# Ten of 22 up-projection pairs as seven half-size products, weight sums on GpSimd, and a first unit fed input by input

## The chip, the cores and the metric

One core of one Trainium2 chip runs the whole program. The metric is the device time of one execution, in microseconds (us). An engine is named as in the profile: PE is TensorE, ACT ScalarE, DVE VectorE, POOL GpSimd, SP the engine that issues the DMAs.

## What is computed

One inference step of a two-layer decoder trunk over 520 token columns: 512 of a prompt and 8 of a sample group. Everything is float32.

```python
def layer(x, ...):
    proj = rmsnorm(x, g_mix) @ w_in            # 1024 -> 5376: u_a v_a q k v gate_a gate_b
    a_out = chunk_spatial_gate(gelu(u_a), rmsnorm(gelu(v_a), g_v), w_s, b_s)
    b_out = merged dilated window attention of q, k, v (three pairs of window and dilation)
    merged = sigmoid(gate_a) * (a_out @ w_a_proj) + sigmoid(gate_b) * (b_out @ w_b_proj)
    x = x + merged @ w_o
    up = rmsnorm(x, g_ffn) @ w_up              # 1024 -> 2 * 2816
    c = conv_b + causal depthwise conv of 3 taps over up
    c_gate, c_val = split(c)
    return x + (silu(c_gate) * c_val) @ w_down # 2816 -> 1024
```

## The kernel before

**Layout and precision.** Activations lie transposed: 128 features on the partitions, 520 tokens along a row, as `x[:, k]` for the eight blocks k of the 1024 features. Each float32 operand of a dense product is split into a high part in the reduced format that PE takes (`act.copy` on ACT) and the rest as a low part (a subtraction on DVE). `triple` (L333) issues three products for one pair of operands, high by high, high by low and low by high, and each for the two halves of the tokens, 260 columns at a time. One output block of 128 features over 1024 inputs takes 8 x 3 x 2 = 48 matmuls; an up pair (one block of values, one of gates) takes 96.

**Order of the work.** `groups` lists the dense products in program order: for each layer the projection of w_in, the gate pairs ("ga", "gb") with w_a_proj and w_b_proj as the loop over j and the tuple `mix` have it, w_o, and then `ffn`: 22 up pairs, with the blocks of w_down for the first three pieces of the hidden features put between them, and the last piece at the end. `loads` and `blocks` follow from it. Weight blocks of 128 x 512 come by DMA into nine `raw` buffers; `split` (L260) makes their high and low parts, in a ring of six (`RING`), as soon as the block six before has been used. Everything else (norm statistics, attention, the gating branch, state columns) is written as generators in lanes; `pump` takes the next step of a lane between matmuls when its due time has come in a running count of PE time. The tile scheduler then fixes each engine's queue; within a queue instructions run in order.

**Norms.** `Norm.feature` splits gain times x into high and low before the norm's factor is known; `Norm.rms` gets that factor from the sums of squares by matmuls with ones (L472), a power on POOL (L137), transposes (L483) and a copy to `rbc`. The factor is multiplied in when a product's accumulators are taken out of PSUM by DVE (`normed` L1142, `copied` L1079). In the first unit, three blocks of layer 0 (`lows_last`), the high weights go first and the low ones last.

**Seven products.** `dense2` (L393) holds a second form for a pair of blocks: two halves of the inputs by two blocks of outputs against two halves of the inputs by two halves of the tokens, as seven products of half size in place of eight, with sums of weight blocks (`summed`, L264, on POOL), sums of normalised inputs (`Norm.operands`), and sums of accumulators when they are taken out. `SEVEN`, the tuple of pairs that take it, is empty, so neither `summed` nor `operands` runs.

**The conv.** `up_conv` (L1378) takes an up block through ACT (L1384) and DVE (L1386, twice, and L1389); `conved` multiplies value and gate and splits the result (L1402, L1403, L568, L569). `a_branch` (L1166) loads the spatial weights w_s and multiplies them by the causal mask (L1172) in its first step.

Of the kernel before, what the change touches and what calls it, by code (L numbers as in the profile page):

```python
# [18 lines left out]
D = 1024  # L19
T = 520  # L20
# [59 lines left out]
NSTD = 3  # L80

SEVEN = ()
# [6 lines left out]
def step_kernel(ctx: ExitStack, tc: tile.TileContext, a, o):  # L89
# [58 lines left out]

    groups = []
# [7 lines left out]
    mix = ("g0", "g1", "b0", "g2", "b1", "b2", "g3", "b3", "b4", "b5", "b6", "b7")  # L157
    for l in range(DEPTH):
# [12 lines left out]
        for p in (2, 1, 0):  # L171
            c = [off + p * 256 + h * 128 for off in (O_Q, O_K, O_VV) for h in range(2)]
            if p == 2:
                n = 3
                one(w_in, 0, 8, *c[:n])
# [9 lines left out]
        for j in range(5):  # L185
            if j < 4:
                two(("ga", j), w_in, O_GA + j * 256, O_GA + j * 256 + 128)
            for i in (2 * j - 2, 2 * j - 1) if j else ():
                one(a["w_a_proj"][l], 0, 4, i * 128)
        for g, j in mix:  # L190
            j = int(j)
            if g == "g":
                two(("gb", j), w_in, O_GB + j * 256, O_GB + j * 256 + 128)
            else:
                one(a["w_b_proj"][l], 0, 2, j * 128)
# [27 lines left out]
    for g, grp in enumerate(groups):  # L223
        if grp[0] == "s":
# [3 lines left out]
            continue  # L228
        _, w, k0, nk, cs = grp
        for k, k1 in steps(nk):  # L230
# [5 lines left out]
          "pin": False}  # L236
    at = {b: i for i, b in enumerate(blocks)}

# [3 lines left out]
    def load_raw():  # L242
# [3 lines left out]
        dma(r[:, :nk], w[k0 * 128 : (k0 + nk) * 128, c0 : c0 + 128].rearrange("(k p) m -> p k m", p=128))  # L246
# [8 lines left out]
    def split(eng=dve):  # L255
# [9 lines left out]
        if groups[g][0] == "u":  # L265
# [12 lines left out]
        with urgent():  # L278
            act.copy(hi[:, :nk], r)  # L279
            eng.tensor_tensor(lo[:, :nk], r, hi[:, :nk].bitcast(F32), op=ALU.subtract)  # L280
# [3 lines left out]
    def feed():  # L284
        while st["split"] < len(blocks) and (st["split"] < RING or st["split"] - RING in st["used"]):
# [21 lines left out]
    def pump(force=False):  # L307

        while True:
            e = [q + [n] for n, k in LANES.items() for q in tasks[n][:k]]  # L310
# [20 lines left out]
    def finish(*lanes):  # L331
        while any(tasks[n] for n in lanes):
            pump(True)  # L333

    def triple(w, x, bank, start, stop, which=(0, 1, 2)):

        pump()
# [15 lines left out]
    def dense(xs, unit, lows_last=False):  # L353
# [7 lines left out]

        def taken(j):
            finish("n")
            with urgent():
                unit(j, *banks[j])

        held = {}
        ks = steps(nk)
        for k0, k1 in ks:
            for j, c in enumerate(cs):  # L370
                held[j, k0] = block(g, (k0, c))
            last = k1 == nk and not lows_last
            for js in [[j] for j in range(len(cs))] if last else [range(len(cs))]:
                for k in range(k0, k1):
                    for j in js:
                        hi, lo = held[j, k0]
                        triple((hi[:, k - k0], lo[:, k - k0]), xs[k], banks[j], k == 0, k == nk - 1,
                               (0, 1) if lows_last else (0, 1, 2))
                if last:
                    used(g, (k0, cs[js[0]]))  # L380
                    taken(js[0])
            if not last and not lows_last:
                for c in cs:
                    used(g, (k0, c))
        for j, c in enumerate(cs) if lows_last else ():
            for k0, k1 in ks:
                feed()
                hi, lo = held[j, k0]
                for k in range(k0, k1):
                    triple((hi[:, k - k0], lo[:, k - k0]), xs[k], banks[j], False, k == nk - 1, (2,))  # L390
                used(g, (k0, c))
            taken(j)

    def dense2(norm, unit, done):
# [5 lines left out]
        while norm.seven and (not norm.xn or (groups[st["g"]][0] == "s" and tasks["x"])):  # L400
            pump(True)
# [38 lines left out]
    class Norm:  # L440


        def __init__(self, gofs, ksum=8):
            self.gofs = gofs
            self.xs = []
            self.ssum = [tmp() for _ in range(2 if ksum < 8 else 1)]
            self.ksum = ksum

        def feature(self, k):
            hi = tmp(T, F32R)  # L450
            lo = tmp(T, F32R)
# [1053 lines left out]
```

## Time and profile before

| | |
|---|---|
| Runs | 1583.2, 1587.14 (median), 1588.96 us |
| Profiled execution | 1582.85 us, of which the span of the trace is 1581.0 us |
| PE matmuls busy | 1558.7 us, 99% of the span, 12985 matmuls |
| DVE busy | 1065.0 us, 67% |
| ACT busy | 713.4 us, 45% |
| POOL busy | 70.9 us, 4% |
| DMA | 164.37 MB, 104 GB/s over the span |

PE is busy throughout, but a matmul's end is modelled and matmuls overlap, so its rate is read from how many of them fit in a stretch rather than from the busy share. The other engines' shares are means over stages that differ much, and a stage is read on its own.

### The profile page before, as it was taken

To read this page: it belongs to the slowest core of one execution; us is meant where nothing else is said; L and a number is where in the kernel's file an instruction comes from. 1 tells how busy PE (TensorE), PEld (TensorE's weight loads), DVE (VectorE), ACT (ScalarE), POOL (GpSimd) and SP (SyncE) were. 2 spreads that over 40 slices of the span, in tenths; PEclk is the share of its full clock that TensorE was granted. 3 is DMA by queue.
4 is the path that set the end of the run, shared out by engine and by line. 5 is a ranking of instruction groups with operands and counts; after the bars stand their busy time and mean duration, and the time that the engine had idled before them with its cause. 6 is when DMAs were issued, how large, how long until landed. Compare 5 with 4: busy or idle time off the path is not lost.

```text
span 1581.0 us, 33056 instructions
## 1 busy us (share of the span) xinstructions
PE 1558.7 (99%) x12985; PEld 1532.2 (97%) x12985; DVE 1065.0 (67%) x2353; ACT 713.4 (45%) x1513; POOL 70.9 (4%) x58
## 2 busy tenths in 40 slices
PE   7999999999999999999999999999999999999999
PEld 6999899999999999999999998999999999999998
DVE  5677868966576665665648686788666766667563
ACT  4564535434454343433545645453444444334342
POOL 0102010000000000000001030100000000000000
PEclk9999999999999999999999999999999999999999
DMA  8343333533323323323344343334333233242321
GB/s 220 110 121 112 108 108 96 162 95 108 87 83 87 101 76 105 96 85 92 102 121 133 94 131 89 112 111 144 94 107 88 78 88 96 83 117 78 101 75 66
DMA packets 299163, 164.37 MB, mean 104 GB/s; under 512 B 18439, under 2 KB 292631, under 8 KB 298991
## 3 DMA queue, kind: packets, MB, share of 16 engines
q1 hardware_dynamic: 299007, 162.26, 35.2%
q8 instruction: 102, 1.67, 0.4%
q14 instruction: 54, 0.44, 0.1%
HBM read 154.66 MB, written 10.36 MB: 104 GB/s over the span
## 4 chain that ended last, share of the span: by engine, by line
PE 95%; DVE 2%; DMA 1%; ACT 1%; SPq 1%; issue 0%; DVEq 0%
PE acc L342 87%; PE tp L843 2%; PE tp L891 1%; PE tp L881 1%; PE tp L800 1%; PE tp L342 1%; PE tp L1239 0%; DVE t L1047 0%; DMA t<-in_x_prompt_dram 0%; PE tp L793 0%; PE tp L826 0%; PE tp L950 0%; PE tp L1214 0%; PE tp L825 0%; DVE t L454 0%
## 5 line engine op out<-in xcount | busy, mean ns | idle before, releaser
L342 PE MATMUL acc<-t,whi 128*128 128x260 f32 x7744 | 1295.5, 285 | 1.4 <-DVE t L1079 1.4
L342 PEld LDWEIGHTS acc<-t,whi 128*128 128x128 f32 x7744 | 1087.6, 189 | 6.9 <-DVE t L1079 2.5
L342 PE MATMUL acc<-t,wlo 128*128 128x260 f32 x3872 | 837.9, 284 | 0.0
L342 PEld LDWEIGHTS acc<-t,wlo 128*128 128x128 f32 x3872 | 619.9, 189 | 2.4 <-issue 0.7
L279 ACT CAST whi<-raw 128x512 fp32r<-128x512 f32 (+2 forms) x536 | 312.0, 583 | 660.4 <-PE acc L342 527.3
L280 DVE TENSOR_TENSOR wlo<-raw,whi 128x512 fp32r<-128x512 f32 (+2 forms) x536 | 341.5, 638 | 170.4 <-ACT whi L279 158.9
L1079 DVE TENSOR_TENSOR t<-acc,t 128x260 f32<-128x260 f32 x296 | 112.5, 421 | 121.9 <-PE acc L342 121.9
L1386 DVE SCALAR_TENSOR_TENSOR t<-t,cwc,t 128x511 f32<-128x511 f32 (+1 forms) x176 | 131.6, 749 | 44.6 <-ACT t L1384 44.4
L1361 DVE TENSOR_TENSOR x<-acc,x 128x260 f32<-128x260 f32 x128 | 48.8, 421 | 37.8 <-PE acc L342 37.7
L1384 ACT ACTIVATE t<-t,vcol,cwc 128x520 f32<-128x520 f32 x88 | 72.1, 819 | 0.0
L137 POOL TENSOR_TENSOR rr<-ss,mhalf 128x8 f32<-128x8 f32 (+1 forms) x30 | 56.2, 1873 | 286.0 <-DVE ss L756 211.8
L569 DVE TENSOR_TENSOR t<-t,t 128x520 fp32r<-128x520 f32 (+1 forms) x84 | 51.8, 617 | 21.7 <-ACT t L568 21.4
L568 ACT CAST t<-t 128x520 fp32r<-128x520 f32 (+1 forms) x84 | 47.3, 563 | 40.5 <-DVE t L1403 18.2
L866 ACT ACTIVATE t<-t,stat 128x128 f32<-128x128 f32 (+1 forms) x96 | 40.0, 419 | 9.1 <-DVE stat L863 8.7
L137 POOL TENSOR_TENSOR rc<-ms,mhalf 128x5 f32<-128x5 f32 x4 | 4.7, 1173 | 748.4 <-DVE ms L477 748.4
L1382 ACT COPY ut<-t 128x10 f32<-128x10 f32 x88 | 18.4, 209 | 34.9 <-DVE t L1079 34.4
L1403 DVE TENSOR_TENSOR t<-t,t 128x520 f32<-128x520 f32 x44 | 30.6, 696 | 1.6 <-ACT t L1402 1.3
L843 PE MATMUL tp<-t 64*128 64x128 f32 x192 | 30.5, 293 | 0.0
L857 DVE TENSOR_TENSOR t<-tp,cst 128x256 f32<-128x256 f32 (+1 forms) x48 | 22.4, 484 | 11.9 <-PE tp L843 11.7
L1402 ACT ACTIVATE t<-t 128x520 f32<-128x520 f32 x44 | 28.1, 639 | 2.2 <-DVE t L1389 0.6
L1363 DVE SCALAR_TENSOR_TENSOR x<-acc,x 128x260 f32<-128x260 f32 x32 | 12.3, 422 | 23.9 <-PE acc L342 23.9
L843 PEld LDWEIGHTS tp<-t 64*128 64x128 f32 x192 | 22.5, 187 | 4.7 <-issue 1.7
(185 smaller groups left out, 996.2 us busy)
## 6 DMA issues: line engine op xcount, KB each, us to landing
raw<-in_w_up_dram SPq DMA_DIRECT2D x176, 256.0 KB
raw<-in_w_in_dram SPq DMA_DIRECT2D x168, 256.0 KB
raw<-in_w_down_dram SPq DMA_DIRECT2D x96, 192.0 KB
t<-in_cache_kv_w_dram SPq DMA_DIRECT2D x48, 256.0 KB
raw<-in_w_o_dram SPq DMA_DIRECT2D x32, 256.0 KB
raw<-in_w_a_proj_dram SPq DMA_DIRECT2D x16, 256.0 KB
raw<-in_w_down_dram SPq DMA_DIRECT2D x32, 128.0 KB
out_dram<-t SPq DMA_DIRECT2D x15, 256.0 KB
```

The lines of the kernel that those rows point to most:

```text
L137: pool.tensor_tensor(out, in_, mhalf[: in_.shape[0], :n], op=ALU.pow)
L279: act.copy(hi[:, :nk], r)
L280: eng.tensor_tensor(lo[:, :nk], r, hi[:, :nk].bitcast(F32), op=ALU.subtract)
L342: mm = pe.matmul(b, wi, xi[:, h * H2 : h * H2 + H2], start=start and i == 0, stop=stop and i == 2,)
L568: act.copy(hi, src)
L569: dve.tensor_tensor(lo, src, hi.bitcast(F32), op=ALU.subtract)
L843: pe.matmul(sc[h2][:, hp * K + s * 128 : hp * K + s * 128 + 128], qkT[rows, hp], kt[rows, 2 + hp], start=True, stop=True,)
L866: act.activation(S[:, hp], S[:, hp], AF.Exp, bias=nmx[:, i : i + 1], accum_out=stat[:, 4 + i : 5 + i])
L1079: dve.tensor_tensor(v2(g)[:, h], acc, n.rb[:, h], op=ALU.mult)
L1361: dve.tensor_tensor(xm, acc, xm, op=ALU.add)
L1384: act.activation(cv, up, AF.Identity, scale=cwc[:, 2, i : i + 1], bias=vcol[:, 32 + i : 33 + i])
L1386: dve.scalar_tensor_tensor(cv[:, s:TP], up[:, : TP - s], cwc[:, j, i : i + 1], cv[:, s:TP], op0=ALU.mult, op1=ALU.add)
```

## The change

`SEVEN` gets the ten up pairs 9, 10, 12, 13, 15, 16, 18, 19, 20 and 21 of each layer, and `NSTD` goes from 3 to 7. In each of these pairs the seven products run, POOL makes four sums of weight blocks, and the splits go from four blocks to seven. `Norm.operands`, which makes the normalised inputs and their sums, runs in steps between the matmuls of the first up pairs; the pairs 7, 8, 11, 14 and 17 use the normalised inputs too, and ACT copies their results out instead of DVE multiplying them.

The first unit of layer 0 (`dense_first`) takes inputs one at a time: the transposes and splits of block k + 1 run while the products of block k - 1 do, and three weight blocks come in one buffer per input. The mask of w_s (L1221, two instructions a layer) comes a step later than its loads, the two lanes of layer 0 start later, and `mix` now orders gate pairs, w_a_proj and w_b_proj in one list.

```diff
-NSTD = 3
-SEVEN = ()
+NSTD = 7
+SEVEN = tuple(("up", i) for i in (9,10,12,13,15,16,18,19,20,21))
+DELAY0 = 1.0
...
-    mix = ("g0", "g1", "b0", "g2", "b1", "b2", "g3", "b3", "b4", "b5", "b6", "b7")
+    mix = "g0 g1 g2 a0 a1 g3 a2 a3 h0 a4 a5 h1 h2 b0 a6 b1 b2 a7 b3 h3 b4 b5 b6 b7".split()
...
+        if grp[0] == "k":
+            loads.extend((grp[1], k, 3, grp[2:]) for k in range(8))
+            blocks.extend((g, k) for k in range(8))
+            continue
...
-    def dense(xs, unit, lows_last=False):
+    def dense(xs, unit):
...
+    def dense_first(feature, norm, unit):
+        st["g"] += 1
+        banks = [[acc_tile(), acc_tile() if j < 2 else tps()[:, :H2]] for j in range(3)]
+        w = []
+        xsq = [tmp(), tmp()]
+        for k in range(8):
+            if 0 < k < 7:
+                for j in range(3):
+                    hi, lo = w[k - 1]
+                    triple((hi[:, j], lo[:, j]), norm.xs[k - 1], banks[j], k == 1, False)
+                used(0, k - 1)
+            st["limit"] = k + 1
+            with tc.high_priority(3 * URGENT):
+                feature(k)
+                w.append(block(0, k))
+                norm.square(k, xsq[k % 2])
+        norm.finish(DELAY0)
+        st["limit"] = 0
+        for j in range(3):
+            for k in (6, 7):
+                hi, lo = w[k]
+                triple((hi[:, j], lo[:, j]), norm.xs[k], banks[j], False, k == 7)
...
+            finish("n")
+            with urgent():
+                unit(j, *banks[j])
...
             if self.seven:
-                add("x", self.operands(), delay + 0.1)
+                add("x", self.operands(), delay + 16.0)
...
-                yield -0.7
+                yield -4.0
...
+    def first_feature(k):
...
+        def columns(k):
+            t = tps()
+            for b in range(4):
+                pe.transpose(t[:, b * 128 : b * 128 + 128], xin[k][:, b], ident)
+            kept(act.copy(x[:, k, :TP], t))
+        if k == 0:
+            columns(0)
+        if k < 7:
+            columns(k + 1)
+        norm.split(k)
...
             for i in range(2):
                 dma(ws[i], a["w_s"][l, 4 * i : 4 * i + 4].rearrange("g t s -> t g s"))
+            yield -4.0
+            for i in range(2):
                 dve.tensor_tensor(
...
-        add("v", a_branch(), 12.0)
-        add("s", attn_samples(), 12.0)
+        add("v", a_branch(), 12.0 if l else 20.0)
+        add("s", attn_samples(), 12.0 if l else 24.0)
```

**PE at the start of the program, before** (L603 transposes inputs, L608 and L613 the sample rows and gains, L342 is the dense product):

```order
L603 MATMUL tp_120<-cst,t_83 128x128 x4
L608 MATMUL tp_126<-cst,t_86 128x8 x4
L608 MATMUL tp_126<-cst,t_87 128x8 x4
L613 MATMUL tp_126<-cst,t_78 128x16
L603 MATMUL tp_151<-cst,t_95 128x128 x4
L603 MATMUL tp_164<-cst,t_97 128x128 x4
L603 MATMUL tp_185<-cst,t_103 128x128 x4
L603 MATMUL tp_198<-cst,t_105 128x128 x4
L342 MATMUL acc_288<-t_138,whi_143 128x260
L342 MATMUL acc_289<-t_138,whi_143 128x260
L342 MATMUL acc_290<-t_138,whi_147 128x260
```

**and with the change** (L658 transposes inputs, L644 and L650 the gains and sample rows, L362 is the dense product):

```order
L644 MATMUL tp_170<-cst,t_78 128x16
L650 MATMUL tp_173<-cst,t_85 128x8 x4
L658 MATMUL tp_179<-cst,t_87 128x128 x4
L658 MATMUL tp_185<-cst,t_95 128x128 x4
L362 MATMUL acc_162<-t_191,whi_195 128x260
L362 MATMUL acc_163<-t_191,whi_195 128x260
L362 MATMUL acc_164<-t_191,whi_195 128x260
L362 MATMUL acc_165<-t_191,whi_195 128x260
L362 MATMUL acc_166<-t_191,whi_195 128x260
L362 MATMUL tp_167<-t_191,whi_195 128x260
L658 MATMUL tp_218<-cst,t_100 128x128 x4
L658 MATMUL tp_252<-cst,t_105 128x128 x4
```

Before, five groups of transposes stand ahead of the first dense matmul; now two do, and the transposes of later inputs follow between the matmuls.

**DVE at the end of the first norm, before** (L462 adds squares, L1172 masks w_s, L280 makes low weights, L476 and L477 begin the norm's factor):

```order
L462 TENSOR_TENSOR t_82<-t_82,t_229 128x520
L462 TENSOR_TENSOR t_82<-t_82,t_242 128x520
L1172 TENSOR_TENSOR t_414<-t_414,cst 128x512
L462 TENSOR_TENSOR t_82<-t_82,t_255 128x520
L1172 TENSOR_TENSOR t_415<-t_415,cst 128x512
L280 TENSOR_TENSOR wlo_436<-raw_294,whi_435 128x512
L280 TENSOR_TENSOR wlo_473<-raw_296,whi_472 128x512
L476 TENSOR_SCALAR ms_394<-tp_388 128x4
L477 TENSOR_SCALAR ms_394<-tp_388 8x1
```

**and with the change** (the same steps are L502, L299, L514 and L515; L493 makes the low part of an input; L1189 takes the first results out):

```order
L493 SCALAR_TENSOR_TENSOR t_419<-x,vcol,t_418 128x520
L299 TENSOR_TENSOR wlo_423<-raw_127,whi_422 128x384
L502 TENSOR_TENSOR t_82<-t_82,t_169 128x520
L299 TENSOR_TENSOR wlo_498<-raw_300,whi_497 128x512
L299 TENSOR_TENSOR wlo_502<-raw_342,whi_501 128x512
L299 TENSOR_TENSOR wlo_506<-raw_378,whi_505 128x512
L299 TENSOR_TENSOR wlo_510<-raw_414,whi_509 128x512
L514 TENSOR_SCALAR ms_448<-tp_442 128x4
L515 TENSOR_SCALAR ms_448<-tp_442 8x1
L512 MEMSET ms_10963 128x1
L1189 TENSOR_TENSOR t_463<-acc_162,t_83 128x260
```

The mask of w_s stood between the last two adds of squares; now it comes after the first results have been taken out.

**DVE where the splits of up pair 10 begin, before** (L280 low weights, L1079 takes a result out, L1386 and L1389 the conv):

```order
L280 TENSOR_TENSOR wlo_7409<-raw_7277,whi_7408 128x512
L280 TENSOR_TENSOR wlo_7443<-raw_7307,whi_7442 128x512
L1079 TENSOR_TENSOR t_7478<-acc_7416,t_5693 128x260
L1079 TENSOR_TENSOR t_7478<-acc_7417,t_5693 128x260
L280 TENSOR_TENSOR wlo_7473<-raw_7348,whi_7472 128x512
L1386 SCALAR_TENSOR_TENSOR t_7481<-t_7478,cwc,t_7481 128x511
L1389 TENSOR_TENSOR t_7481<-t_7481,hc_280 128x8
L1386 SCALAR_TENSOR_TENSOR t_7481<-t_7478,cwc,t_7481 128x510
L280 TENSOR_TENSOR wlo_7514<-raw_7366,whi_7513 128x512
L1079 TENSOR_TENSOR t_7549<-acc_7487,t_5693 128x260
L1079 TENSOR_TENSOR t_7549<-acc_7488,t_5693 128x260
L280 TENSOR_TENSOR wlo_7544<-raw_7394,whi_7543 128x512
```

**and with the change** (`sum` tiles come from POOL; L457 and L462 take a half-size product out with a sum):

```order
L299 TENSOR_TENSOR wlo_7554<-sum_7397,whi_7553 128x512
L457 TENSOR_TENSOR t_7538<-acc_7558,t_7538 128x260
L299 TENSOR_TENSOR wlo_7580<-raw_7354,whi_7579 128x512
L457 TENSOR_TENSOR t_7538<-acc_7592,t_7538 128x260
L299 TENSOR_TENSOR wlo_7606<-sum_7573,whi_7605 128x512
L457 TENSOR_TENSOR t_7539<-acc_7610,t_7538 128x260
L299 TENSOR_TENSOR wlo_7624<-raw_7407,whi_7623 128x512
L457 TENSOR_TENSOR t_7539<-acc_7628,t_7539 128x260
L299 TENSOR_TENSOR wlo_7642<-sum_7575,whi_7641 128x512
L462 TENSOR_TENSOR t_7539<-acc_7646,t_7539 128x260
L463 TENSOR_TENSOR t_7538<-acc_7646,t_7538 128x260
L299 TENSOR_TENSOR wlo_7660<-raw_7405,whi_7659 128x512
```

**and POOL's four sums for that pair** (before, POOL has nothing here), with the first of the next:

```order
L281 TENSOR_TENSOR sum_7571<-raw_7403,raw_7405 128x512
L281 TENSOR_TENSOR sum_7573<-sum_7571,raw_7354 128x512
L281 TENSOR_TENSOR sum_7575<-raw_7354,raw_7403 128x512
L281 TENSOR_TENSOR sum_7577<-raw_7407,sum_7573 128x512
L281 TENSOR_TENSOR sum_8028<-raw_7890,raw_7920 128x512
```

The splits of pair 10 run while the products of pair 9 are taken out, and three of every seven low parts that DVE makes there read a tile that POOL has just written.

## Rows read from the trace of the kernel before

**Rows 1.** The chain of waits of the whole span: shares by line, and its longest piece (start, length).

```profile
by line: PE acc L342 87.1%; PE tp L843 1.9%; PE tp L891 1.0%; PE tp L881 0.7%; PE tp L800 0.7%; PE tp L342 0.7%; PE tp L1239 0.5%; issue 0.4%; DVE t L1047 0.4%; DMA t<-in_x_prompt_dram 0.3%; PE tp L793 0.3%; PE tp L826 0.3%; PE tp L950 0.3%
...
435.49 333.95 PE acc L342 x2784
```

**Rows 2.** Windows of chosen stretches: length, busy us (instructions) by engine, granted clock, DMA share, GB/s.

```profile
34.00:42.00 8.00, 7.92 (x40) 7.71 (x40) 3.95 (x9) 1.47 (x3) 1.20 (x1) 0.57 0.45 128
...
180.00:200.00 20.00, 16.62 (x147) 13.90 (x148) 15.66 (x33) 10.42 (x30) 0.00 (x0) 1.00 0.27 70
...
435.50:769.40 333.90, 333.90 (x2786) 333.90 (x2786) 217.15 (x438) 139.95 (x263) 0.00 (x0) 1.00 0.31 90
```

**Rows 3.** Timeline of PE, first 44 us: start, length, instruction, count [idle before].

```profile
8.19 2.08 PE L603 MATMUL tp<-cst,t 128*128 128x128 f32 x8 [1.86 <-DMA t<-in_x_prompt_dram]
...
13.54 3.60 PE L342 MATMUL acc<-t,whi 128*128 128x260 f32 x15
16.93 1.33 PE L603 MATMUL tp<-cst,t 128*128 128x128 f32 x8
...
20.95 1.00 PE L342 MATMUL tp<-t,whi 128*128 128x260 f32 x7
...
34.08 1.49 PE L472 MATMUL tp<-ones,t 128*128 128x1 f32 x10 [2.91 <-DVE t L462]
...
40.87 0.87 PE L483 MATMUL tp<-cst,rc 128*128 128x128 f32 x4
...
42.56 1.15 PE L1195 MATMUL tp<-cst,t 128*128 128x128 f32 x8
43.47 0.49 PE L342 MATMUL acc<-t,whi 128*128 128x260 f32 x2
```

**Rows 4.** Timelines of ACT and DVE in the same stretch.

```profile
5.87 0.62 ACT L279 CAST whi<-raw 128x512 fp32r<-128x512 f32 x1 [3.87 <-DMA raw<-in_w_in_dram]
...
32.63 0.69 DVE L1172 TENSOR_TENSOR t<-t,cst 128x512 f32<-128x512 f32 x1 [6.18 <-DMA t<-in_w_s_dram]
...
42.92 1.43 DVE L1142 TENSOR_TENSOR t<-acc,t 128x260 f32<-128x260 f32 x4
```

**Rows 5.** Groups by form, whole span: busy us, mean ns of one, idle before.

```profile
L342 PE MATMUL acc<-t,whi 128*128 128x260 f32 x7744 | 1295.5, 285 | 1.4 <-DVE t L1079 1.4
...
L280 DVE TENSOR_TENSOR wlo<-raw,whi 128x512 fp32r<-128x512 f32 x392 | 268.3, 685 | 115.7 <-ACT whi L279 105.7 <-PE acc L342 1.8 <-issue 1.5
...
L1079 DVE TENSOR_TENSOR t<-acc,t 128x260 f32<-128x260 f32 x296 | 112.5, 421 | 121.9 <-PE acc L342 121.9
...
L1386 DVE SCALAR_TENSOR_TENSOR t<-t,cwc,t 128x511 f32<-128x511 f32 x88 | 66.1, 751 | 44.6 <-ACT t L1384 44.4
...
L569 DVE TENSOR_TENSOR t<-t,t 128x520 fp32r<-128x520 f32 x68 | 47.3, 696 | 21.0 <-ACT t L568 20.6
...
L453 ACT ACTIVATE t<-x,vcol 128x520 fp32r<-128x520 f32 x32 | 23.3, 728 | 4.7 <-DVE x L1363 2.5 <-DVE x L1361 1.9 <-DVE x L604 0.3
```

**Rows 6.** Groups by form on POOL, whole span.

```profile
L137 POOL TENSOR_TENSOR rc<-ms,mhalf 128x5 f32<-128x5 f32 x4 | 4.7, 1173 | 748.4 <-DVE ms L477 748.4
...
L673 POOL TENSOR_TENSOR sS<-cst,gs 32x32 f32<-32x32 f32 x4 | 1.3, 352 | 0.0
...
L670 POOL TENSOR_TENSOR sC<-cst,gs 32x64 f32<-32x64 f32 x2 | 0.8, 398 | 0.3 <-POOL gs L667 0.3
```

**Rows 7.** Timelines of POOL and of DVE around 150 us.

```profile
149.38 1.75 POOL L137 TENSOR_TENSOR rr<-ss,mhalf 128x8 f32<-128x8 f32 x1 [0.81 <-DVE ss L715]
153.32 6.38 POOL L137 TENSOR_TENSOR rr<-ss,mhalf 128x8 f32<-128x8 f32 x1 [2.19 <-DVE ss L715]
...
153.83 0.68 DVE L280 TENSOR_TENSOR wlo<-raw,whi 128x512 fp32r<-128x512 f32 x1
154.43 0.69 DVE L1258 SCALAR_TENSOR_TENSOR t<-t,t 128x520 f32<-128x520 f32 x1
...
158.13 0.75 DVE L1079 TENSOR_TENSOR t<-acc,t 128x260 f32<-128x260 f32 x2
```

More of the change, by code (lines that the diff above doesn't have):

```diff
@@ L263, in summed @@
             return s
-        if groups[g][0] == "u":
+        if groups[g][0] != "s":
             r = next_raw()
@@ L284, in feed @@
     def feed():
-        while st["split"] < len(blocks) and (st["split"] < RING or st["split"] - RING in st["used"]):
+        while st["split"] < (st["limit"] or len(blocks)) and (st["split"] < RING or st["split"] - RING in st["used"]):
             split()
@@ L360, in dense @@
         banks = [[acc_tile(), acc_tile() if j < 2 else tps()[:, :H2]] for j in range(len(cs))]
[L362 to L365, printed above, removed]
         held = {}
-        ks = steps(nk)
-        for k0, k1 in ks:
+        for k0, k1 in steps(nk):
             for j, c in enumerate(cs):
                 held[j, k0] = block(g, (k0, c))
-            last = k1 == nk and not lows_last
+            last = k1 == nk
             for js in [[j] for j in range(len(cs))] if last else [range(len(cs))]:
@@ L376, in dense @@
                         hi, lo = held[j, k0]
-                        triple((hi[:, k - k0], lo[:, k - k0]), xs[k], banks[j], k == 0, k == nk - 1,
-                               (0, 1) if lows_last else (0, 1, 2))
+                        triple((hi[:, k - k0], lo[:, k - k0]), xs[k], banks[j], k == 0, k == nk - 1)
                 if last:
                     used(g, (k0, cs[js[0]]))
-                    taken(js[0])
-            if not last and not lows_last:
+                    finish("n")
+                    with urgent():
+                        unit(js[0], *banks[js[0]])
+            if not last:
                 for c in cs:
                     used(g, (k0, c))
[L385 to L392, printed above, removed]
+    def dense_first(feature, norm, unit):
[20 more added lines that the diff above has]
+                triple((hi[:, j], lo[:, j]), norm.xs[k], banks[j], False, k == 7)
+            if j == 2:
+                used(0, 6)
+                used(0, 7)
+            finish("n")
+            with urgent():
+                unit(j, *banks[j])
     def dense2(norm, unit, done):
@@ L583, in step_kernel @@
     norm = Norm(0)
+    norm.prepare()
     xin = []
+    dma(cst[:, :128], a["cst"][:, :128])
+    xrow = [tmp(512) for _ in range(2)]
     for k in range(8):
@@ L1126, in unit @@
                 have(first[0] + j, g)
-            dense(xs, unit, l == 0)
-            if l == 0:
+            if l:
+                dense(xs, unit)
+            else:
+                dense_first(first_feature, norm, unit)
                 t = tps()
```

193 lines of the change are left out of this document (95 added, 98 removed).

## The prediction

> **What bounds the kernel now.** I read the chain of waits first: the dense product's line alone is 87.1% of the span, and its longest piece is 2784 matmuls in 333.95 us without a break [rows 1]. That is 0.120 us a matmul, the rate on which every term below rests. The windows come next. The stretch of that piece is the up projection of layer 0 with the down blocks in it, and there PE is busy for all of 333.9 us, DVE for 217.15 and ACT for 139.95 [rows 2]. So PE's count sets the time, and the others have room. Last, the timeline of the start: the first dense matmul runs at 13.54 us and the fourth unit begins only at 43.47 [rows 3]. In between DVE waits 6.18 us for w_s [rows 4], with the last add of squares queued behind it; PE stands still for 2.9 us until that add is done [rows 3], and in the 8 us after that its granted clock is 0.57 on average, so mostly at the lower level, 1.2 GHz [rows 2].
>
> **The seven products.** A pair falls from 96 matmuls to 7 x 12 = 84. The matmul's shape stays 128x260, and all twelve of a product go to one bank; seven in a row to one bank took 1.00 us [rows 3], and with 0.285 for the last [rows 5] that is 0.715 / 6 = 0.119 between starts, so one bank costs nothing extra. 12 x 0.120 = 1.44 us a pair, and 20 pairs give **-28.8 us**. Nothing is added on PE.
>
> **What the other engines get, by layer.** DVE makes three more low parts a pair: 30 x 0.685 = 20.6 us. It takes out seven half-size results instead of four, 30 more, while the pairs 7, 8, 11, 14 and 17 give 20 to ACT: 10 x 0.421 = 4.2 us. The operands cost 8 normalisations at 0.75 (as L1386, also a multiply by a scalar and a second operation on a tile), 16 low parts of 520 columns at 0.696 and 16 sums of 260 at 0.421: 6.0 + 11.1 + 6.7 = 23.8 us. That is 48.6 us [rows 5], and DVE would have 217.2 + 48.6 = 265.8 us in a stretch of 333.9 - 14.4 = 319.5, 83%. ACT has 180 us to spare [rows 2] and even 50 more leave it under 60%. The weights' bytes stay the same. So on average PE still covers it all.
>
> **POOL.** No row shows POOL adding 128x512. Two small forms differ by 46 ns for 32 columns [rows 6]: 1.44 ns a column, and 0.352 + 480 x 0.00144 = 1.04 us an add as an estimate. Four make 4.2 us a pair. Where the pair before has down blocks ahead of it, its weights are there early and PE covers this. The tight places are the three pairs of neighbours in a layer with no down block between, 9 and 10, 15 and 16, 20 and 21, because the second's sums wait for the first's to be used.
>
> What DVE and POOL do to each other is the unknown. A power on POOL that takes 1.75 us took 6.38 us while DVE ran back to back [rows 7]. DVE did not slow: its instructions there start 0.60 us apart, for a length of 0.68. POOL finished after DVE's two L1079, which read one operand from PSUM, had come by. So I take it that POOL gets in at such an instruction, that it then delays DVE by what is left of its add, and that a dense DVE comes first. A pair costs DVE 7 x 0.685 + 7 x 0.421 + 4 x 0.751 + 2 x 0.696 = 12.1 us by lengths [rows 5], and by starts (0.60 for 0.68) some 10.7. Two neighbours are 21.4 us. Eight adds, each with 1.04 - 0.38 us beyond a result that is being taken out, add 5.3: 26.7 against 20.2 us of PE. The six blocks of the ring lead by 6 x 1.44 = 8.6 us, which is more than 6.5. The ends are 0 and, with DVE's lengths and no overlap at all, (24.2 + 8.3 - 20.2 - 8.6) x 6 = 22 us. I take **+2 us**, near the lower end, because the only row on it shows DVE keeping pace.
>
> The Trainium skill (SBUF - State Buffer, "Who interferes with whom") says that a DVE instruction with two SBUF inputs contends with a GpSimd instruction that reads SBUF, and that whichever starts first has the port for its whole length while the other fully blocks. The trace agrees on the one side, POOL blocked by DVE (6.38 us against 1.75), and shows nothing on the other, a DVE instruction that POOL blocks. By the rule DVE's splits and conv steps would stand still for each add, and the time would be the first rival's below, 1576 us; by the row it is the forecast's.
>
> **The operands' steps** are put off by 16 us and spread with 4.4 us between them, five and six of them. Their 23.8 us of DVE lie in the pairs 0 to 8, where DVE has a third free. They hold 32 of the 61 buffers that everything shares; a step that waits for a buffer would show as idle DVE, which costs PE nothing until the ring is used up. I cost it at 0.
>
> **The start.** With the change the first weights stand at the same place in SP's queue as before, so they land by 5.87 us [rows 4]; but ACT copies input 1 ahead of the first split, and the second input's transposes began at 8.19 us before [rows 3]. Transposes, copy and two splits of input 0 then put the first dense matmul at about 10.7, instead of 13.54. PE's work from there is 144 matmuls x 0.120 = 17.3, six groups of four transposes at 1.33 / 2 = 4.0, and 1.7 lost while the rate is low (fifteen took 3.60 instead of 1.9) [rows 3]: 23.0 us, to 33.7. ACT's four instructions an input, none over 0.728 [rows 5], make at most 23.3 us, the same. The norm follows: sums 1.5 [rows 3], power 1.17 [rows 6] with an estimated 0.5 around it, from the transposes at 40.87 [rows 3] to the first results at 42.92 [rows 4] 2.05: 5.2 us, of which seven matmuls cover 0.8. The fourth unit starts at about 38, 5.4 earlier, less the 1.15 of L1195 that was done by then and now comes later [rows 3]: **-4 us**. The mask of w_s no longer stands ahead of the last adds; behind it now is nothing of the norm. Ends: 0, if the inputs come one after another with nothing overlapped, and -8, if the norm's 5.2 us are mostly hidden.
>
> **The order of the gate pairs** moves the same matmuls about. PE's idle time there is 3.4 us at 180 to 200 [rows 2], and as much in layer 1 at most; the attention steps that it waits for also start later. I take 0, between -7 and +7.
>
> **Sum.** -28.8 + 2 - 4 = -30.8 us. The profiled execution had a span of 1581.0 us and took 1582.85; with the change 1550.2 and 1552.1. The median shown is 4.3 us above that execution, so the forecast of a median is 1587.1 - 30.8 = **1556 us**.
>
> **Rivals.**
> *The lock holds at the neighbours (1576 us, 0.17).* Each add stops DVE for its whole length, and the 22 us above are lost at the six neighbour places: -28.8 + 22 - 4 = -10.8. That is what the section of the Trainium skill named above would make of it. For it: every split reads two SBUF tiles, and POOL's share is there in every pair. Against it: DVE kept its pace beside the power.
> *The sums come late in every pair (1608 us, 0.11).* POOL waits for a gap in a dense DVE, as it did for 4.63 us at 153 us. The sum S2 is made from the sum S1, so two such waits in a row make 2 x (1.04 + 4.63) = 11.3 us, and the ring covers 8.6. ACT stands at the high part of S2 with all later splits behind it, and PE waits 2.7 us in each of 20 pairs: 54 us, less the 32.8 of the products and the start, +21. It decides from 1.6 us a pair. Against it: while ACT waits, DVE runs dry and lets POOL in.
> *The start gains nothing (1560 us, 0.08).* The inputs' chain of transposes, copy and splits is as long as what it replaces. It lies inside the forecast's own range.
> The forecast itself has 0.60, and what is left, 0.04, lies between the first two rivals.
>
> **Range and chances.** The ends of the terms give 1587 - 28.8 - 8 - 7 = 1543 and, for the first rival with its start at 0 and the order at +3, 1583. I take 1544 to 1583; the late sums lie outside it, and so does some of the tails. A measurement of this kernel tells about 0.5%, 8 us, from no change. Faster by more (below 1579): the forecast, the third rival and three quarters of the first, 0.81. Within it: 0.08. Slower: 0.11.
>
> **What would show it.** The matmul rate in the up stretch stays at 0.120 us, its stretch is some 14 us shorter, and PE shows no gaps there: the products are right. POOL's adds last 1.0 to 1.3 us and DVE's low parts keep 0.69: the +2 is right. If DVE's splits show lengths of 1 us and more, or PE waits for ACT's high part of a sum in the second of two neighbours, it is the first rival; gaps in single pairs too, the second. The first dense matmul near 10.7 us and the fourth unit near 38 would show the start right. I am wrong if the up stretch is not shorter by at least 5 us in each layer.

## The result, and the profile after

The changed kernel takes **1577.19 us** (median of 7 runs, 1574.72 to 1580.67) against 1585.66 for the kernel before on the same chip: a ratio of 0.995, 95% interval 0.9937 to 0.9962. The forecast was 1556. The direction was right and the time lies in the range, but of the 30.8 us that the sum gave, 8.5 came. The traces below are of single executions, of 1582.85 us before (2.8 below the median) and 1577.19 after, so they differ by less than the medians.

The matmuls fell as forecast, from 12985 to 12745. DVE's busy time grew by 131 us, of which the sum by lengths had 97:

```profile
PE 1537.3 (98%) x12745; PEld 1508.1 (96%) x12745; DVE 1195.7 (76%) x2507; ACT 781.1 (50%) x1676; POOL 196.3 (12%) x138
```

PE's busy time fell by 21.4 us (from 1558.7) and the span by only 5.8 (1581.0 to 1575.2): PE now stands still for 37.9 us instead of 22.3. Windows of layer 0 show where, first before, then after. They run from the first matmul of one stage to that of the next: start to the fourth unit, the gates and projections up to w_o, up to the place of the first seven-product pair, and from there to the last down blocks. The gates' stretch begins behind the first two gate pairs, up to which the order is the same.

```profile
0.00:43.47 43.47, 32.69 (x209) 30.72 (x210) 24.84 (x47) 19.60 (x34) 3.35 (x11) 0.92 0.78 212
...
247.94:370.32 122.38, 121.62 (x1037) 119.41 (x1036) 94.56 (x269) 55.20 (x134) 0.00 (x0) 1.00 0.40 118
...
416.26:550.43 134.17, 134.17 (x1121) 133.94 (x1120) 88.90 (x181) 59.82 (x112) 1.17 (x1) 1.00 0.31 90
550.43:763.53 213.10, 213.10 (x1779) 213.10 (x1777) 132.98 (x268) 84.70 (x159) 0.00 (x0) 1.00 0.31 90
```

```profile
0.00:37.27 37.27, 28.36 (x202) 26.83 (x202) 18.04 (x38) 21.91 (x43) 4.72 (x11) 0.95 0.73 206
...
243.84:369.34 125.50, 123.17 (x1037) 120.81 (x1036) 95.09 (x271) 54.49 (x134) 0.00 (x0) 0.99 0.39 115
...
415.43:552.24 136.81, 134.57 (x1122) 133.92 (x1120) 109.91 (x212) 70.55 (x136) 9.32 (x7) 1.00 0.30 87
552.24:756.84 204.60, 199.87 (x1659) 198.86 (x1658) 179.43 (x314) 105.33 (x209) 53.68 (x35) 1.00 0.33 93
```

The first number after the window is its length, the second PE's busy time. Of [rows 2] the up stretch had no idle PE at all. Now the gates take 3.1 us more, the first up pairs 2.6 more, and the stretch of the seven-product pairs is 8.5 us shorter where 14.4 were due, with 4.7 us of idle PE. Layer 1 shows the same (3.3, 3.3, and 8.0 shorter), and its w_in stage takes 1.8 more. At the start 43.47 has become 37.27; behind the first two gate pairs 4.1 us of that are left (243.84 against 247.94). The up stretch as a whole is 5.9 us shorter in layer 0 and 4.7 in layer 1; the forecast said that it would be wrong if either were under 5.

PE's waits after, in us in total, times, and the longest:

```profile
PE acc L362 <- ACT t L465: 7.6, 6, 1.7
PE acc L362 <- DVE t L1189: 5.0, 4, 1.7
...
PE tp L619 <- DMA t<-in_conv_w_dram: 2.3, 1, 2.3
PE acc L362 <- DVE t L1378: 2.1, 1, 2.1
```

L465 copies the result of product "11", the first of the seven. L1189 takes out an ordinary pair; it is L1079 of [rows 5]. L619 and L1378 wait in the gates, one in each layer. None of these is a wait that the forecast named.

Groups by form, which answer to [rows 5, 6]:

```profile
L299 DVE TENSOR_TENSOR wlo<-raw,whi 128x512 fp32r<-128x512 f32 x366 | 258.1, 706 | 98.2 <-ACT whi L298 95.2 <-DMA t<-in_cache_kv_w_dram 1.3
L1432 DVE SCALAR_TENSOR_TENSOR t<-t,cwc,t 128x511 f32<-128x511 f32 x88 | 78.6, 894 | 22.0 <-ACT t L1430 21.8
...
L281 POOL TENSOR_TENSOR sum<-raw,raw 128x512 f32<-128x512 f32 x40 | 61.3, 1532 | 485.2 <-DMA raw<-in_w_up_dram 328.7 <-DVE wlo L299 100.8 <-DVE t L462 21.1
L299 DVE TENSOR_TENSOR wlo<-sum,whi 128x512 fp32r<-128x512 f32 x80 | 58.7, 737 | 16.8 <-ACT whi L298 16.6
L457 DVE TENSOR_TENSOR t<-acc,t 128x260 f32<-128x260 f32 x100 | 41.6, 423 | 7.4 <-PE acc L362 5.4 <-issue 0.4
```

An add on POOL takes 1.53 us in the mean of the forty shown, not 1.04. DVE's low parts rise from 685 to 706 and 737 ns and its conv steps from 751 to 894; taking a result out of PSUM (L457) stays at 423, as L1079 had 421. So DVE's instructions do get longer beside POOL's adds. Whether that costs time is a question for the runs. The 80 low parts of sums in 20 pairs also show that four of a pair's seven low parts read what POOL made, not three as the text on the change has it.

**One wait followed back.** Pair 15 follows pair 14 with no down block between. PE, ACT, DVE and POOL around 650 us:

```profile
654.78 0.51 PE L362 MATMUL acc<-t,whi 128*128 128x260 f32 x2 [1.67 <-ACT t L465]
```

```profile
650.76 0.64 ACT L1448 ACTIVATE t<-t 128x520 f32<-128x520 f32 x1
651.61 0.63 ACT L298 CAST whi<-raw 128x512 fp32r<-128x512 f32 x1 [0.21 <-PE acc L362]
653.31 0.62 ACT L609 CAST t<-t 128x520 fp32r<-128x520 f32 x1 [1.08 <-DVE t L1449]
653.84 0.61 ACT L298 CAST whi<-sum 128x512 fp32r<-128x512 f32 x1
654.36 0.37 ACT L465 COPY t<-acc 128x260 f32<-128x260 f32 x1
```

```profile
649.62 0.74 DVE L1432 SCALAR_TENSOR_TENSOR t<-t,cwc,t 128x510 f32<-128x510 f32 x1
650.28 1.79 DVE L299 TENSOR_TENSOR wlo<-raw,whi 128x512 fp32r<-128x512 f32 x1
651.99 0.68 DVE L299 TENSOR_TENSOR wlo<-sum,whi 128x512 fp32r<-128x512 f32 x1
652.59 0.69 DVE L1449 TENSOR_TENSOR t<-t,t 128x520 f32<-128x520 f32 x1
```

```profile
649.83 1.69 POOL L281 TENSOR_TENSOR sum<-raw,sum 128x512 f32<-128x512 f32 x1 [1.37 <-issue]
```

Pair 15 begins at 645.77, so product "11", twelve matmuls, is done by 647.5. Its copy starts at 654.36, 7 us later. A bank is a buffer in PSUM that holds one product's result until it is taken out. The program gives five to the products and three to the transposes. Five banks at 1.44 us each are full before the copy comes, so the sixth product stands still until the copy has freed the first bank. The copy stands in ACT's queue behind L609, which splits the product of pair 14, and that waits for pair 14's conv and L1449 on DVE. One low part in that chain, at 650.28, took 1.1 us longer than the next, while POOL's add ran. Two causes are thus in one picture: the queue, with work of the pair before ahead of the copy, and POOL.

### The profile page after: what moved, and what is told of

It is laid out like the page before. It is cut to its first block, busy times and chain, and to the rows that moved or that the text cites. A ratio compares the mean times of both kernels' runs of the same rounds, so it can differ in the third digit from the quotient of the medians.

```text
span 1575.2 us, 33158 instructions
## 1 busy us (share of the span) xinstructions
PE 1537.3 (98%) x12745; PEld 1508.1 (96%) x12745; DVE 1195.7 (76%) x2507; ACT 781.1 (50%) x1676; POOL 196.3 (12%) x138
## 5 line engine op out<-in xcount | busy, mean ns | idle before, releaser
L362 PE MATMUL acc<-t,whi 128*128 128x260 f32 x7584 | 1306.1, 286 | 18.2 <-ACT t L465 7.6
L362 PEld LDWEIGHTS acc<-t,whi 128*128 128x128 f32 x7584 | 1094.7, 189 | 26.7 <-ACT t L465 9.2
L362 PE MATMUL acc<-t,wlo 128*128 128x260 f32 x3792 | 880.0, 285 | 0.0
L362 PEld LDWEIGHTS acc<-t,wlo 128*128 128x128 f32 x3792 | 633.9, 189 | 2.4 <-issue 0.7
L298 ACT CAST whi<-raw 128x512 fp32r<-128x512 f32 (+2 forms) x518 | 299.1, 579 | 481.8 <-PE acc L362 348.1
L299 DVE TENSOR_TENSOR wlo<-raw,whi 128x512 fp32r<-128x512 f32 (+2 forms) x518 | 351.7, 680 | 119.8 <-ACT whi L298 116.3
L1432 DVE SCALAR_TENSOR_TENSOR t<-t,cwc,t 128x510 f32<-128x510 f32 (+1 forms) x176 | 146.1, 841 | 22.0 <-ACT t L1430 21.8
L281 POOL TENSOR_TENSOR sum<-raw,raw 128x512 f32<-128x512 f32 x40 | 61.3, 1532 | 485.2 <-DMA raw<-in_w_up_dram 328.7
L1124 DVE TENSOR_TENSOR t<-acc,t 128x260 f32<-128x260 f32 x144 | 54.7, 419 | 34.9 <-PE acc L362 34.9
L298 ACT CAST whi<-sum 128x512 fp32r<-128x512 f32 x80 | 49.6, 620 | 61.2 <-PE acc L362 61.1
L609 ACT CAST t<-t 128x520 fp32r<-128x520 f32 (+1 forms) x84 | 47.2, 563 | 54.7 <-DVE t L1449 31.6
L1407 DVE TENSOR_TENSOR x<-acc,x 128x260 f32<-128x260 f32 x128 | 48.8, 419 | 31.8 <-PE acc L362 31.1
L299 DVE TENSOR_TENSOR wlo<-sum,whi 128x512 fp32r<-128x512 f32 x80 | 58.7, 737 | 16.8 <-ACT whi L298 16.6
L457 DVE TENSOR_TENSOR t<-acc,t 128x260 f32<-128x260 f32 x100 | 41.6, 423 | 7.4 <-PE acc L362 5.4
L1189 DVE TENSOR_TENSOR t<-acc,t 128x260 f32<-128x260 f32 x76 | 29.2, 421 | 16.8 <-PE acc L362 14.9
L281 POOL TENSOR_TENSOR sum<-sum,raw 128x512 f32<-128x512 f32 x20 | 32.7, 1635 | 19.9 <-issue 19.0
```

Of the source, the lines that this page charges most:

```text
L281: pool.tensor_tensor(s, p, q, op=op)
L298: kept(act.copy(hi[:, :nk], r))
L299: kept(dve.tensor_tensor(lo[:, :nk], r, hi[:, :nk].bitcast(F32), op=ALU.subtract))
L362: mm = pe.matmul(b, wi, xi[:, h * H2 : h * H2 + H2], start=start and i == 0, stop=stop and i == 2,)
L457: return lambda acc: dve.tensor_tensor(out, acc, p, op=ALU.add)
L609: act.copy(hi, src)
```

## The experiments

Theory 1 was that POOL's hold on DVE makes the waits (the first rival, whose 1576 us is near the time measured). Theory 2 was that the copy is late by its place in the queue.

**Without POOL's sums.**

```diff
-                d["S1"] = summed(d["21"], d["22"], ALU.add)
-                d["S2"] = summed(d["S1"], d["11"], ALU.subtract)
-                d["S3"] = summed(d["11"], d["21"], ALU.subtract)
-                d["S4"] = summed(d["12"], d["S2"], ALU.subtract)
+                d["S2"] = d["S3"] = d["21"]
+                d["S1"] = d["S4"] = d["22"]
```

> Leaves out the sums of weight tiles on GpSimd: the products S1 to S4 multiply tile 21 or 22 as it is, so POOL runs no L281 and everything else of the change stays. Theory 1 (GpSimd's adds stop DVE, and DVE's lateness makes the waits at the neighbour pairs): DVE's low parts go back to 0.685 us, the up stretch of each layer loses its waits for L465 and L1407 (about 5 us a layer), and the time is about 10 us below the changed kernel, 1567 us. Theory 2 (the copy of the first product's result stands in ACT's queue behind the pair before, whatever GpSimd does): the waits for L465 stay and the time is within 3 us of the changed kernel's 1577.

1574.34 us, 0.9935 (0.9921 to 0.9949) of before. DVE's pace is what theory 1 says; the time is theory 2's. The waits for the copy (L463 here) stay at 6.0 of 7.6 us, those for ordinary pairs (L1187) at 5.0. What goes is half of pair 15's wait (0.86 instead of 1.67 us in layer 0, and the same in layer 1) and the two waits for L1407, 0.9 us each; pairs 16 and 21 wait as long as with the sums. Groups, PE's waits, and the window of the seven-product pairs:

```profile
L297 DVE TENSOR_TENSOR wlo<-raw,whi 128x512 fp32r<-128x512 f32 x446 | 306.0, 687 | 129.0 <-ACT whi L296 122.4 <-DMA t<-in_cache_kv_w_dram 2.7
L1430 DVE SCALAR_TENSOR_TENSOR t<-t,cwc,t 128x511 f32<-128x511 f32 x88 | 65.8, 748 | 28.2 <-ACT t L1428 28.0
```

```profile
PE acc L360 <- ACT t L463: 6.0, 6, 1.4
PE acc L360 <- DVE t L1187: 5.0, 4, 1.7
```

```profile
552.00:757.00 205.00, 201.98 (x1678) 201.20 (x1677) 159.10 (x318) 108.26 (x214) 0.00 (x0) 1.00 0.33 95
```

POOL's hold makes some 20 us of DVE time in this stretch (179.8 us of 205 with the sums), and 2.8 us of the whole program, which is little more than the scatter (the intervals of the two ratios overlap).

**No seven-product pair next to another.**

```diff
-SEVEN = tuple(("up", i) for i in (9,10,12,13,15,16,18,19,20,21))
+SEVEN = tuple(("up", i) for i in (8,9,11,12,13,15,17,18,19,21))
```

> Still ten seven-product pairs a layer, but 8, 9, 11, 12, 13, 15, 17, 18, 19, 21, so that no two of them follow each other without down blocks or an ordinary pair between. Theory 1 and 2 alike (the loss is at the neighbours): 15/16 and 20/21 together lost 3.5 + 1.0 us and the pair 14 1.2 us a layer, so some 9 us are won against the changed kernel, about 1568 us. Rival (DVE is full at 88% in the whole stretch, so the waits only move): within 3 us of 1577.

1591.88 us, 1.0039 (1.0027 to 1.0052): slower than before; both theories missed, and so did the rival. The wait for L465 grew:

```profile
PE acc L362 <- ACT t L465: 12.5, 6, 2.5
```

In layer 0 it stands in the pairs 11, 15 and 17, which took 14.37, 11.99 and 13.82 us instead of 10.1 (first matmul to the next unit's). Each follows an ordinary pair directly. In 11 and 17 the granted clock fell as well, as pair 11's window shows (PEclk 0.88):

```profile
574.79:589.32 14.53, 12.00 (x88) 11.80 (x87) 12.08 (x19) 6.29 (x15) 5.98 (x4) 0.88 0.30 86
```

The waits for L465 grew by 4.9 us, the time by 14.7. Most of the rest is the clock: its mean in the profiled execution is 0.988 against 0.994 for the changed kernel, by estimate some 10 us (0.006 x 1590). Of the pairs behind down blocks only 8, the first, loses more than 0.6 us (1.2). So it is not two seven-product pairs side by side that matter, but a pair of either kind just ahead, with no down block between. That is not the whole condition: pair 21 here and pair 10 in the changed kernel also follow a pair directly and lost only 0.1 and 0.2; what spares them was not tried.

**The order of the gate units as before.**

```diff
-    mix = "g0 g1 g2 a0 a1 g3 a2 a3 h0 a4 a5 h1 h2 b0 a6 b1 b2 a7 b3 h3 b4 b5 b6 b7".split()
+    mix = "g0 g1 a0 a1 g2 a2 a3 g3 a4 a5 a6 a7 h0 h1 b0 h2 b1 b2 h3 b3 b4 b5 b6 b7".split()
...
                     finish("v")
-                    add("v", history())
                 gated(m1[j], As)
+                if j == 7:
+                    add("v", history())
```

> The changed kernel with the gate units and the two projections back in the order of before, and the conv history behind the last of the first projection. Theory (the new order costs the 3.1 and 3.3 us that the stretch between the first projection and w_o grew by, in waits for the conv weights' transfer and for DVE): about 6 us less than the changed kernel, 1571 us. Rival (the stretch grew because the clock falls there once a layer for 3.41 us, whatever the order): 1577 with the falls still there, or half of it, 1574, if only the waits go.

1571.08 us, 0.9911 (0.9897 to 0.9925): 6.1 us won, as the theory said. The gates of layer 0 take 122.1 us again, and the falls of the clock are gone there as well. About half of what they had grown by was the clock: of the 3.1 us, PE's idle time has 1.6, and its busy time for the same 1037 matmuls the other 1.6. Whether the order of the units or the place of the conv history does it was not tried.

**The start and the order of the gates alone.**

```diff
-NSTD = 7
-SEVEN = tuple(("up", i) for i in (9,10,12,13,15,16,18,19,20,21))
+NSTD = 3
+SEVEN = ()
```

> The changed kernel without any seven-product pair (and so without operands and sums; the normalised inputs are still not made, as before): the start and the order of the gate units alone. By the stage times of the two traces: start -4.1, order +6.4, one fall of the clock +1.7, so about 4 us above the kernel before, 1590 us. By the terms of the forecast: -4 and 0, 1582 us.

1586.84 us, 1.0014 (1.0005 to 1.0023) of the 1584.48 beside it: +2.4, between the two figures. With 6.1 for the order, if the two add, the start gives -3.7. All that the seven products bring in the changed kernel is 1586.84 - 1577.19 = 9.7 us.

**The copy on DVE.**

```diff
-        product("11", 1, lambda acc: act.copy(a11, acc))
+        product("11", 1, lambda acc: dve.tensor_copy(a11, acc))
```

> The changed kernel with the first product's result taken out by DVE instead of ACT (L465), nothing else. Theory 1 (the copy is late because it stands in ACT's queue behind L609, the split of the pair before, which waits for DVE): PE's six waits for L465, 7.6 us, and the waits that follow from them go, about 1569 us. Rival (the same work of the pair before stands in DVE's queue too, and DVE is what is late): the waits come back under a DVE line and the time is within 3 us of 1577.

1585.53 us, 0.9999 (0.999 to 1.0008): 8 us worse than the changed kernel, so the rival's time is missed as well. Its cause holds: the work of the pair before stands ahead of the copy on DVE too, and the waits there are more and longer (up to 2.4 us).

```profile
PE acc L362 <- DVE t L465: 12.2, 8, 2.4
```

**The operands' steps cut in two.** Each step then handles one input of the two, with `yield -1.8` between.

> The changed kernel with each step of the normalised inputs cut into two, one input's multiply and high part and one other's low part at a time, with half the pause between; the number of instructions is the same. Theory (a step issues two multiplies and two low parts, 2.8 us of DVE in a row, and so L1189, the taking out of an ordinary pair, comes 1.7 us late): PE's waits for L1189, 5.0 us, go and the stretch from up to the first seven-product pair is 2.6 and 3.3 us shorter in the two layers, about 1571 us. Rival (DVE has too much to do in these pairs, however it is cut): 1577 us with as much waiting, at more places.

1579.09 us, 0.9964 (0.995 to 0.9977): nothing won. PE waits for the same line (L1192 here) 5.3 us in six places instead of 5.0 in four. The rival holds: DVE has too much to do in so short a stretch, however it is cut.

**Seven products only behind down blocks.**

```diff
-SEVEN = tuple(("up", i) for i in (9,10,12,13,15,16,18,19,20,21))
+SEVEN = tuple(("up", i) for i in (9,12,13,14,18,19,20))
```

> Only the seven pairs 9, 12, 13, 14, 18, 19, 20 a layer, each of which directly follows down blocks. Theory 1 (the loss of a seven-product pair is that of a pair that directly follows another, of either kind): no wait for L465, each of the 14 pairs gives its 1.44 us, 20.2 us off the kernel without sevens (1.0014 of before), and the operands' early steps cost their 5.9 us: 1584.5 + 2.4 - 20.2 + 5.9 = about 1573 us, less than with ten. Rival (each seven-product pair gives only 9.7 / 20 = 0.49 us, wherever it stands): 1586.8 - 6.8 = 1580 us.

1573.38 us, 0.9929 (0.9916 to 0.9941), and PE waits for no copy. Seven pairs a layer bring more than ten.

**Eight banks instead of five.**

```diff
-            acc = acc_tile()
+            acc = tps()[:, :H2] if name in ("11", "S2", "12") else acc_tile()
```

> The changed kernel with the products 11, S2 and 12 of a seven-product pair accumulated in the three PSUM banks that the transposes use, which idle in this stretch, instead of in the five of the products: PE can run three products (4.3 us) further ahead of the copy L465. Theory 1 (the copy is only late, by up to 1.7 us, while DVE and ACT have time over the pair as a whole): the waits for L465 go and the time is about 1569 us. Rival (DVE, 88% busy in the stretch, is what is short there): the waits come back at other lines, within 3 us of 1577.

1568.84 us, 0.9899 (0.9886 to 0.9913): 8.3 us less. The copy of pair 15 still starts 8.6 us after the pair's first matmul (655.23 and 646.64; 654.36 and 645.77 in the changed kernel), behind the same L609. DVE is busy as before, and PE is not waiting:

```profile
552.00:757.00 205.00, 204.83 (x1706) 204.42 (x1705) 182.02 (x323) 108.92 (x217) 54.20 (x35) 1.00 0.33 96
```

**The operands' steps further apart.**

```diff
-                yield -4.0
+                yield -9.0
```

> The changed kernel with the five steps of the normalised inputs left whole but some 10 us apart instead of 4.4; they still end before the first pair that reads them. Theory (the steps put 11.5 us of DVE into 21 us of pairs that already take two thirds of DVE, however they are cut; over 50 us there is room): PE's waits for L1189, 5.0 us, go or fall to under 1.5, and the time is about 1572 us. Rival (L1189 is late behind each single step of four instructions, so five steps cost the same at any distance): 1577 us.

1573.09 us, 0.992 (0.9906 to 0.9933): 4.1 us won, and no wait for L1189 is left among PE's longest. In the changed kernel DVE had worked through a step's low parts just ahead of it, and PE stood for 1.72 us:

```profile
460.65 1.30 DVE L556 TENSOR_TENSOR t<-t,t 128x520 fp32r<-128x520 f32 x2
461.87 0.75 DVE L1189 TENSOR_TENSOR t<-acc,t 128x260 f32<-128x260 f32 x2
```

```profile
462.34 0.51 PE L362 MATMUL acc<-t,whi 128*128 128x260 f32 x2 [1.72 <-DVE t L1189]
```

**Three edits together**: the old order, eight banks, steps further apart.

> The changed kernel with three of the edits together: the old order of the gate units, the products 11, S2 and 12 in the transposes' banks, and the steps of the normalised inputs 10 us apart. If the three losses are separate places of the program, they add: 1577 - 6 - 8 - 5 = 1558 us, near the 1556 that was forecast for the change itself. If they share a cause (DVE full), the sum is not reached and it stays at 1563 or more.

**1554.6 us**, 0.9801 (0.9788 to 0.9815): faster than both kernels, and at the forecast's time. The losses add; the sum of the three is 18.5 us, and 22.6 were won. Much of the surplus is scatter of the medians: in the profiled executions the three win 7.2, 8.9 and 5.3 us by themselves, 21.4, and 23.0 together. The clock, which in this execution falls nowhere after the start, can be the rest. In a window of the seven-product pairs PE is idle for 0.45 us:

```profile
540.00:750.00 210.00, 209.55 (x1747) 208.94 (x1746) 186.49 (x329) 112.19 (x224) 55.70 (x36) 1.00 0.33 96
```

**Thirteen pairs on top of that**, `range(9, 22)`.

> The kernel with the three edits and seven products in all pairs from 9 to 21, 13 a layer instead of 10. If PE's count sets the time, six more pairs give 6 x 1.44 = 8.6 us, 1549 us. If DVE is the end (182 us of 205 in the stretch of the kernel with the banks alone, and each further pair adds some 5 us to it), DVE is at 97% there, waits come back at its lines, and the time is that of the kernel with ten, 1558 us, or more.

1578.95 us, 0.9955 (0.9941 to 0.9969): 24 us worse than ten. DVE is late here. PE's waits and a window:

```profile
PE acc L362 <- DVE t L457: 9.4, 2, 5.2
PE acc L362 <- ACT whi L298: 4.9, 3, 1.7
...
PE acc L362 <- DVE wlo L299: 4.3, 3, 1.6
```

```profile
550.00:760.00 210.00, 198.90 (x1607) 197.46 (x1606) 195.22 (x340) 106.12 (x207) 68.37 (x45) 0.97 0.31 91
```

DVE is busy for 195.22 of 210 us. Most of the waits are for its results, in part for weights (L299) and in part for banks again: L457 takes out a result whose bank PE needs next. Around the longest wait of layer 0, behind the pairs 9, 10 and 11 in a row:

```profile
573.09 1.58 POOL L281 TENSOR_TENSOR sum<-sum,raw 128x512 f32<-128x512 f32 x1
573.44 3.49 DVE L1433 SCALAR_TENSOR_TENSOR t<-t,cwc,t 128x510 f32<-128x510 f32 x2
576.85 1.23 DVE L1436 TENSOR_TENSOR t<-t,hc 128x8 f32<-128x8 f32 x1
583.42 0.80 PE L362 MATMUL acc<-t,whi 128*128 128x260 f32 x2 [4.20 <-DVE t L457]
```

The four adds for pair 12 run here from 571.61 to 578.06. Beside them two conv steps take 3.49 us and an 8-column add 1.23; at 561.58 and 560.89 one of each takes 0.74 and 0.16. So POOL's hold is in this lateness, and no run shows thirteen pairs without the sums. The loss is also more than the waits: the mean clock of the profiled execution is 0.989 against 0.997 with ten pairs, by estimate some 12 of the 24 us (0.008 x 1578).

**Eight banks, and no sums.**

> The products 11, S2 and 12 in the transposes' banks, and the sums on GpSimd left out (S1 to S4 multiply tile 21 or 22 as it is): the price of GpSimd's adds where the banks no longer make PE wait. DVE's busy time in the stretch falls by some 20 us, as without the sums alone. If that is all cover, the time is that with the banks, 1569 us, within 2. If the adds' hold on DVE costs PE time as the first rival of the forecast has it, it falls well below, to 1560 us or less.

1566.5 us, 0.9881 (0.9868 to 0.9895): 2.3 us less than with the banks alone, again with overlapping intervals. The same window as with the banks:

```profile
552.00:757.00 205.00, 205.00 (x1711) 205.00 (x1711) 161.98 (x323) 109.43 (x216) 0.00 (x0) 1.00 0.33 96
```

DVE's 182.02 us have become 161.98, and PE has 0.17 us less idle time. With ten pairs and the banks, then, POOL's hold costs nearly nothing: DVE's 20 us a layer are not on the path.

## Why the prediction was wrong

**Seven products, -28.8.** Right in itself. A seven-product pair that does not wait takes 10.1 us (84 x 0.120), and with the three edits all of them do: the stretch from the first such pair to the last down blocks, 213.1 us before, takes 199.4.

**"On average PE still covers it all": the step that failed.** The forecast summed the busy times of DVE and ACT, and they came out near: 265.8 us of DVE were forecast for the up stretch of layer 0, and 289.3 came (109.91 + 179.43, over a slightly longer stretch and with POOL's hold of some 20 in it). From that it concluded that PE has no gaps. But with five banks each result must also be out of its bank within some 6 us (4 x 1.44), and in both engines' queues the conv, the silu and the split of the pair before stand ahead of it. "One bank costs nothing extra" was true of the matmuls and said nothing of when the bank comes free. Price: **8.3 us**, by the run with eight banks. The Trainium skill (Perfetto Trace Analysis, "Matmul Optimizations") asks for all eight PSUM banks to be in use, and that run, 8.3 us faster with eight in use here than with five, agrees.

**"I cost it at 0", the operands' steps.** The forecast spread their 23.8 us over the pairs 0 to 8, where DVE had a third free. The inputs' own 11.5 us fall into some 20 us, where PE waits for an ordinary pair's results. Price: **4.1 us**, by the run with the steps apart.

**The order of the gates, 0 between -7 and +7.** It is **+6.1**, inside its ends, and 0 was the wrong value to take. The waits there are for DVE (L1378) in layer 1 and, in layer 0, of a transpose of conv weights (L619), which the profile puts down to their transfer here and to a DVE step in three other runs. About half of the 6.1 is the clock that falls behind them.

**POOL, +2.** Removing the sums saves 2.8 us, or 2.3 with more banks: the size was right, within the scatter, and the reason was not, so that was luck. By the forecast's own signs (adds of 1.0 to 1.3 us, low parts that keep 0.69) the +2 would have failed, and low parts of 1 us and more, which came, would have spoken for the first rival. The forecast held that a dense DVE goes first and keeps its pace. It does not: POOL's adds make DVE's instructions longer by up to a fifth on average. The rule of the Trainium skill that the forecast weighed against the row (SBUF - State Buffer, "Who interferes with whom") was the better guide to what happens; the trace agrees with it in the low part of 1.79 us beside the add of 1.69, and in L457, which has one input in PSUM and kept its 423 ns. The first rival, built on it, gave 1576 us and would have been taken for the cause by its time alone. The run without sums refutes its price: with ten pairs, what POOL takes from DVE is mostly time that DVE had to spare.

**The start, -4.** Measured -3.7. The first dense matmul ran at 9.87 us (10.7 forecast), the fourth unit at 37.27 (38). That is 6.2 us earlier, and some of the agreement is luck: 1.5 of the 2.1 us that were lost again went in the fourth unit (7.35 us instead of 5.83), which now begins while the clock is still low. The forecast had no such term.

```profile
37.00:45.00 8.00, 8.00 (x55) 8.00 (x55) 4.05 (x10) 5.23 (x11) 0.00 (x0) 0.77 0.93 256
```

**The sums late in every pair** (1608): not seen; PE waits for no high part of a sum, and behind down blocks the seven-product pairs of the changed kernel do not wait at all.

Together: -28.8 - 4 + 2 were forecast; 8.3 for the banks, 4.1 for the steps and 6.1 for the order were not. That makes -12.3, and -8.5 came. The 3.8 left over are near the error of the differences, and falls of the clock are part of them. With the three losses taken out, 1554.6 against 1585.85 us for the kernel before beside it is -31.3, so the three terms that were forecast hold together.

## What to carry to other kernels

A form that needs fewer matmuls hands PE's results over more often: count for each result how long its bank may stay full and what stands ahead of its copy in that engine's queue, not only each engine's busy time. Where the copy is late and not the engine short, more banks win the time back; where the engine is nearly full (DVE at 93%, POOL's hold included), eight were not enough, and fewer of the cheap products were faster than all. When one experiment's time fits a rival, take the rival's cause away before believing it: the time fitted here, and the cause gave 2.8 us of the 22 it was priced at.

## What the runs showed of the hardware

The granted clock fell to the lower level, 1.2 GHz, in three short stretches in which it had not fallen in the trace before, each right behind idle PE. Windows of 4 us of the changed kernel, around two of them:

```profile
960.00:964.00 4.00, 2.88 (x27) 1.96 (x25) 3.11 (x8) 2.45 (x13) 0.00 (x0) 1.00 0.22 66
964.00:968.00 4.00, 3.27 (x20) 2.85 (x20) 2.38 (x6) 1.93 (x7) 0.00 (x0) 0.71 0.08 8
...
1064.00:1068.00 4.00, 1.95 (x18) 1.78 (x17) 4.00 (x13) 0.71 (x2) 0.00 (x0) 1.00 0.93 295
1068.00:1072.00 4.00, 4.00 (x23) 4.00 (x22) 4.00 (x12) 1.85 (x4) 0.00 (x0) 0.57 1.02 344
```

At 1064 PE was idle for 2.05 us, in the wait for L1378, and then ran at a clock of 0.57 with 23 matmuls in 4 us instead of some 36. So a gap costs more than its length. At 960, in the w_in stage, the change moves nothing, and the kernel before has the same gaps at the same work and keeps its clock:

```profile
966.00:970.00 4.00, 2.92 (x31) 2.34 (x29) 4.00 (x11) 1.83 (x9) 0.00 (x0) 1.00 0.24 69
970.00:974.00 4.00, 3.22 (x25) 2.48 (x26) 2.55 (x7) 2.62 (x11) 0.00 (x0) 1.00 0.08 9
```

That is the 1.8 us by which w_in of layer 1 grew. Why one falls there and the other doesn't, no run here tells. It is not settled by the program alone: executions of the kernel before, beside the later runs, took from 1581.23 us at a mean clock of 0.999 to 1588.56 at 0.994.

So a difference of a few us between two kernels can be clock in part. The mean clock of the profiled executions was 0.994 for the changed kernel, 0.997 with the old order and with the three edits, 0.991 with the copy on DVE, and 0.988 and 0.989 in the two runs whose waits grew most.
